# Splitting the first load of an im2col kernel into 2 KB and 6 KB per partition, both ahead of the opening barrier

## The chip, the cores and the metric

The kernel runs on one core of one Trainium2 chip. The metric is device time in microseconds (us), as a median of several executions. The profile's span is shorter than that time by 1.8 us. The rounds ran on different chips; the kernel before had medians of 91.27 to 91.48 us in all of them. "ScalarE" is the engine that the profile calls ACT, "VectorE" is DVE, "SyncE" is SP; SyncE issues every transfer of this kernel. A load or the store of one channel is 128 packets, one for each partition; in the traces sixteen are under way at a time, one on each of sixteen DMA engines, and each engine takes eight.

Times of packets, here, in the prediction and in the expectations, are counted from the trace's last packet of the kind "instruction", which comes 0.07 to 0.09 us ahead of the profile's zero. To compare one of them with a time of the timelines, take off that much.

## The reference

The reference copies every 3 x 3 patch of an input of 16 x 64 x 32 x 32 float32 numbers into columns. Each output row is one shifted 30 x 30 window of one input channel, so the kernel does no arithmetic.

```python
for b in range(batch):
    col_idx = 0
    for i in range(h_out):
        for j in range(w_out):
            patch = x[b, :, i:i + kernel_size, j:j + kernel_size].copy()
            cols[b, :, col_idx] = patch.ravel()
            col_idx += 1
```

It reads 4.19 MB and writes 33.18 MB.

## The kernel before

Each of the 128 partitions holds eight channels of one image, 32 KB. Row r of the flat view below is 32 numbers, or 128 bytes; channel 0 is rows 0 to 31. The first load brings channels 0 and 1 (8 KB a partition), the second the other six (24 KB).

```python
first = load(nc.sync, 0, 2 * H)
load(nc.sync, 2 * H, CPP * H)
...
for c in range(0, CPP, 2):
    out_tile = out_pool.tile([P, 2, KK, HO, WO], x.dtype, name="out_tile")
    for s in range(2):
        for kk in range(KK):
            ki, kj = divmod(kk, K)
            src = in_tile[:, c + s, ki : ki + HO, kj : kj + WO]
            dst = out_tile[:, s, kk]
            if kk % 3 != 1 if c + s == 0 else on_act[n % len(on_act)]:
                nc.scalar.copy(out=dst, in_=src)
            else:
                nc.vector.tensor_copy(out=dst, in_=src)
            n += 1
        if c == 0:
            nc.sync.dma_start(out=out_v[:, s], in_=...)   # one store per channel
    if c > 0:
        nc.sync.dma_start(out=out_v[:, c : c + 2]..., in_=...)
```

So ScalarE copies six of the nine windows of channel 0, and the first store goes out when these and VectorE's three are done. After the program is built, the first load is moved ahead of the barrier that opens the program, at which the engines wait for each other before their own work starts:

```python
at = next(k for k, i in enumerate(head)
          if i.engine == load.engine and type(i).__name__ == "InstDrain")
head.insert(at, load)
```

Nothing in the source mentions ScalarE's table load (the instruction ACT_TABLE_LOAD in the profile). The compiler inserts it in front of ScalarE's first copy.

## Time and profile before

| | before |
|---|---|
| time, median of 6 | 91.30 us (91.22 to 91.51) |
| span of the profiled execution | 89.5 us |
| DMA queue busy | 97.2% of sixteen engines' span |
| VectorE, ScalarE busy | 25%, 31% |
| table load on ScalarE | 0.79 to 2.07 us |
| first copy, first store issued | 4.74 us, 9.92 us |

The lines themselves are in the prediction.

### The profile page before, as it was taken

How to read it: one execution, taken by the hardware profiler on the slowest of the kernel's cores; microseconds unless marked ns; L12 is line 12 of the kernel's file. 1: busy time of each engine (PE TensorE's matmuls, PEld its weight loads, DVE VectorE, ACT ScalarE, POOL GpSimd, SP SyncE). 2: the span in 40 equal slices, each digit the busy share in tenths (PEclk: the TensorE clock that was granted, in tenths of full speed). 3: DMA queues.
4: the chain of work that ended last, by engine and by line, in shares of the span. 5: the costliest groups of instructions: out<-in, count | busy, mean ns of one | idle time of the engine just before them, and what ended most of it. 6: DMA issues, size and time to landing. Idle time of an engine off the chain costs nothing.

```text
span 89.5 us, 136 instructions
## 1 busy us (share of the span) xinstructions
DVE 22.4 (25%) x41; ACT 27.7 (31%) x32; POOL 0.2 (0%) x4
## 2 busy tenths in 40 slices
DVE  0089369900000099400000499200000000000000
ACT  5089999910000099900000499200000000000000
POOL 0000000000000000000000000000000000000000
DMA  5989899999989999996699999999999996779990
GB/s 146 498 373 505 351 463 463 463 463 434 405 376 405 695 463 463 463 405 290 290 405 463 463 463 463 463 463 463 463 463 463 463 463 290 318 318 463 463 463 0
DMA packets 1008, 37.37 MB, mean 417 GB/s; under 512 B 112, under 2 KB 112, under 8 KB 112
## 3 DMA queue, kind: packets, MB, share of 16 engines
q1 hardware_dynamic: 1008, 37.37, 97.2%
HBM read 4.19 MB, written 33.18 MB: 417 GB/s over the span
## 4 chain that ended last, share of the span: by engine, by line
DMA 41%; ACT 15%; DVE 6%; DVEq 1%; issue 0%
DMA out_dram<-out_tile 36%; ACT out_tile L54 15%; DVE out_tile L56 6%; DMA in_tile<-in_x_dram 5%; DVEq L82 1%; DVEq L56 0%
## 5 line engine op out<-in xcount | busy, mean ns | idle before, releaser
L54 ACT COPY out_tile<-in_tile 128x900 f32<-128x900 f32 x31 | 26.5, 938 | 28.0 <-DMA out_dram<-out_tile 25.4
L56 DVE COPY out_tile<-in_tile 128x900 f32<-128x900 f32 x41 | 22.4, 624 | 34.2 <-DMA out_dram<-out_tile 27.1
L54 ACT ACT_TABLE_LOAD x1 | 1.3, 1283 | 0.8 <-PEq L111 0.8
L111 POOL MEMSET const-bfloat16-1.0<- 128x1 bf16 x1 | 0.1, 102 | 0.0
L111 POOL MEMSET const-uint8-127<- 128x1 uint8 x1 | 0.1, 102 | 0.0
L111 POOL MEMSET const-float32-1.0<- 128x1 f32 x1 | 0.1, 99 | 0.0
L111 POOL MEMSET const-float32-0.0<- 128x1 f32 x1 | 0.1, 98 | 0.2 <-issue 0.2
## 6 DMA issues: line engine op xcount, KB each, us to landing
out_dram<-out_tile SPq DMA_DIRECT2D x3, 8100.0 KB, 32.1
out_dram<-out_tile SPq DMA_DIRECT2D x2, 4050.0 KB, 15.3
in_tile<-in_x_dram SPq DMA_DIRECT2D x1, 3072.0 KB, 11.2
in_tile<-in_x_dram SPq DMA_DIRECT2D x1, 1024.0 KB, 4.7
```

Source lines behind the costliest of these rows:

```text
L54: nc.scalar.copy(out=dst, in_=src)
L56: nc.vector.tensor_copy(out=dst, in_=src)
L82: tc.compile()
L111: nc = _bacc.Bacc("TRN2", target_bir_lowering=False, num_devices=1)
```

## The change

The intent is to have a small first piece land sooner, so that work can begin sooner, with both pieces issued ahead of the barrier.

```diff
-    first = load(nc.sync, 0, 2 * H)
-    load(nc.sync, 2 * H, CPP * H)
+    cuts = [0, 16, 2 * H, CPP * H]
+    first = [load(nc.sync, r0, r1) for r0, r1 in zip(cuts[:2], cuts[1:3])]
+    load(nc.sync, cuts[2], cuts[3])
...
-    load = first.ins
...
+    for load in (f.ins for f in first):
...          # each is moved ahead of the barrier, in this order
```

More of the change, by code (lines that the diff above doesn't have):

```diff
@@ L83 @@
     blocks = tc.nc.main_func.blocks
-    load = first.ins
-    home = next(b for b in blocks if any(i.name == load.name for i in b.instructions))
-    home.instructions = [i for i in home.instructions if i.name != load.name]
-    head = list(blocks[0].instructions)
-    at = next(
-        k
-        for k, i in enumerate(head)
-        if i.engine == load.engine and type(i).__name__ == "InstDrain"
-    )
-    head.insert(at, load)
-    blocks[0].instructions = head
+    for load in (f.ins for f in first):
+        home = next(
+            b for b in blocks if any(i.name == load.name for i in b.instructions)
+        )
+        home.instructions = [i for i in home.instructions if i.name != load.name]
+        head = list(blocks[0].instructions)
+        at = next(
+            k
+            for k, i in enumerate(head)
+            if i.engine == load.engine and type(i).__name__ == "InstDrain"
+        )
+        head.insert(at, load)
+        blocks[0].instructions = head
 _INS = ['x', 'kernel_size']
```

## The prediction

> **What bounds the kernel now.** I began with the page, at its rows over time and its DMA queue, because a kernel that moves 4.19 MB in and 33.18 MB out and computes nothing but copies is most likely bound by transfers.
>
> ```profile
> DVE  0089369900000099400000499200000000000000
> ACT  5089999910000099900000499200000000000000
> DMA  5989899999989999996699999999999996779990
> q1 hardware_dynamic: 1008, 37.37, 97.2%
> ```
>
> The reader is to see that VectorE and ScalarE are idle most of the time, that one queue carries everything, and that its packets fill 97.2% of sixteen engines' span. A digit below 9 in the DMA row is not a hole: packets are booked where they end, so slices with few ends look poor. To find real holes I read the timeline of the first 25 us and the DMA issues.
>
> ```profile
> 0.00 1.12 SPq L35 DMA_DIRECT2D in_tile<-in_x_dram  x2
> 0.79 1.28 ACT L54 ACT_TABLE_LOAD   x1 [0.79 <-PEq L111]
> 4.74 13.60 ACT L54 COPY out_tile<-in_tile 128x900 f32<-128x900 f32 x16 [2.67 <-DMA in_tile<-in_x_dram]
> 4.74 4.93 DVE L56 COPY out_tile<-in_tile 128x900 f32<-128x900 f32 x9 [4.74 <-DMA in_tile<-in_x_dram]
> 9.92 2.87 SPq L59 DMA_DIRECT2D out_dram<-out_tile  x2
> 18.36 0.33 SPq L64 DMA_DIRECT2D out_dram<-out_tile  x1
> ...
> in_tile<-in_x_dram SPq DMA_DIRECT2D x1, 3072.0 KB, 11.2
> in_tile<-in_x_dram SPq DMA_DIRECT2D x1, 1024.0 KB, 4.7
> ```
>
> The first load (8 KB a partition, 1024 KB) is issued at 0.00 and has landed at 4.71. The second (24 KB a partition) is issued at about 0.79 and lands 11.2 later, at 12.0. ScalarE loads its table from 0.79 to 2.07 while it would have to wait for the first load anyway, and then copies. The first store is issued at 9.92, when six ScalarE copies and three VectorE copies of channel 0 are done: the issuing queue waited for ScalarE, since VectorE needs only 3 x 0.62 us. The single packet records of the trace complete the picture: the first packet of the first load starts at 1.116 and its last one ends at 4.448; the packets of the second load run out, engine by engine, between 11.285 and 11.717; the first packet of the first store starts at 11.291; the last packet of the last store ends at 88.31. In each DMA engine one packet starts where the one before it ended, across all seven transfers.
>
> So the span is 1.12 (issue to first packet) + 87.19 (engines never empty) + 1.2 (receipt and closing barrier) = 89.5 us. A saving must start the first packet earlier or make packets faster. A loss arises as soon as the queue runs dry, and the place where that is nearest is the seam between the second load and the first store. The store is issued at 9.92. On an empty queue the first load took 1.116 from issue to first packet, so the store could have started at 9.92 + 1.12 = 11.04; the first engine is free at 11.29. The slack is 0.25 us.
>
> **What the Trainium skill says.** "DMA: Bandwidth & Descriptors", section "Issuing engines are not separate DMA queues": all transfers interleave on the same 16 engines. The trace agrees: transfers follow each other without a hole, so cutting one of them adds no bandwidth. The same page, "Latency and other measured facts", gives some 600 ns to the first byte on this path; the trace has 1.116 us for the first load, and I use the trace, with the page's figure as the favourable end. "ScalarE: Activation LUTs", section "What ACT_TABLE_LOAD costs", gives 1283 ns for the table load and a further drain of about 1380 ns for a switch:
>
> ```profile
> L54 ACT ACT_TABLE_LOAD x1 | 1.3, 1283 | 0.8 <-PEq L111 0.8
> ```
>
> The 1283 ns agree. Whether a drain follows the load cannot be seen here, because the engine waits for data after it. "Perfetto Trace Analysis", section "Identifying Dependency Chains", says that an instruction which waits for several engines may get EventSemaphore instructions in front of it with the other conditions. The program before has none ahead of the first ScalarE copy; the changed program has one, and that decides my prediction.
>
> **The change part by part.** (1) It adds one issue on SyncE ahead of the opening barrier: 0.38 us from the two issue durations of the line (0.332 and 0.382). The barrier and the issue of the 24 KB load come some 0.36 us later, at about 1.15 instead of 0.79. The queue still has the first 8 KB to move until 4.45, so this is hidden.
>
> (2) It adds 128 packets and 16 completion packets. A 24 KB packet takes 914 ns, an 8 KB packet 309 ns once running: 3 x 309 - 914 is 13 ns for two more packets, so some 6 ns each. Each engine gets 8 more: 0.05 us, plus 0.01 for its completion packet. I put 0.1 us on the landing of all loads: the 6 KB piece lands at 4.8, the 24 KB load is out of the engines from 11.39.
>
> (3) It does not let a copy start sooner. The first copies read rows 0 to 29 of channel 0; the small piece holds rows 0 to 15. So both engines' first copies wait for both pieces, and the last bytes that they need come no earlier than before.
>
> (4) It moves a wait. In the instruction order of the changed program the first ScalarE copy has two loads to wait for. The wait for the 6 KB piece has become an instruction of its own, and it stands ahead of the table load; the copy itself keeps only the wait for the 2 KB piece. Before, the table load waits for nothing but the barrier, and the copy for the load. So the 1.28 us of table load, which lay inside the wait of 4.74, now come after the landing. ScalarE starts copying at 4.8 + 0.05 + 1.28 = about 6.1, against 4.74.
>
> (5) The first store follows ScalarE. From first copy to issue took 9.92 - 4.74 = 5.18 us; that stays. So it is issued at 6.1 + 5.18 = 11.3, and with 1.12 to the first packet it starts at 12.4, while the first engine is empty at 11.39. The hole is 1.0 us with 1.12 of latency, 0.5 us with the page's 0.6. I take 0.9. The slack of 0.25 is eaten before it: delay 1.36 less 0.25 is 1.1, plus or minus the 0.1 by which the loads themselves end later, which is the same sum.
>
> (6) A restart may ramp. The first load's packets took 369 ns on average against 309 in the steady state, eight to an engine: 0.48 us lost. A store into HBM need not do the same; I put 0.05 to 0.1 on it.
>
> (7) Later stores are not on the path. The second is issued at 12.5 + 1.3 = 13.8 and the engines have the first one until about 22; the third goes from 18.36 to 19.7 with work until about 31. Both later output tiles are released by stores and get the same shift.
>
> Sum: 0.1 for the packets, 0.9 for the hole, 0.1 for the restart: 1.1 us on 91.28, so 92.4.
>
> **The rivals.** Hidden or neutral, 91.3: the table load might be executed ahead of the wait all the same, or the engines' queues might hold enough. For it speaks that a 97% busy queue hides most things; against it that the wait is an instruction in ScalarE's own order and that the seam has only 0.25 us of slack. A small gain, 91.0: smaller first packets could get through the slow ramp at the start (500 to 900 ns for many of the first 8 KB packets) faster. For it speaks that this ramp costs 0.48 us; against it that the bytes are the same and that the first packet cannot start before 1.12. A long table switch, 93.7: if the drain of 1.38 us follows the table load before the first copy, the hole grows to 2.3 us. Against it speaks that no drain stands in the program between the two. A double loss at the start: if the second piece's descriptors come too late, the small piece (256 KB, 0.6 us at the steady rate) is through before them. The second issue lies 0.38 us behind the first, so its first packet can start at 1.5, and the small piece lasts till 1.7 at the earliest: no hole, 0.1 at worst.
>
> **Range and chances.** The sum is 1.1 with about 0.5 us of uncertainty from the latency and 0.3 from the restart; the neutral rival has perhaps one chance in ten and sets the lower end, the drain rival also one in ten and sets the upper. Two per cent is 1.83 us, so slower needs 93.1. A gain of 2% would need 1.8 us out of a start that has 1.1 before the first packet: almost excluded. I give 92.4, 91.6 to 93.1.
>
> **What would show it right or wrong.** In the profile after, the table load should start at about 4.8, released by a load, and the first ScalarE copy at about 6.1; VectorE's first copy should stay at 4.7 to 4.9. The first store should be issued at about 11.3, and the fine windows from 11.4 to 12.4 should show engines with nothing to do. All later landings should be shifted by the same 1 us. If the table load still starts near 1 us, step 4 is wrong; if it is late and no hole appears, steps 5 and 6 are; if ScalarE starts a microsecond or more after the table load's end, the drain is real.

## The result, and the profile after

| | before | after |
|---|---|---|
| time, median of 6 | 91.30 us (91.22 to 91.51) | 92.65 us (92.21 to 93.01) |
| span of the profiled execution | 89.5 us | 90.4 us |

The ratio is 1.0146, with a 95% interval of 1.0114 to 1.0177. Ratios here are worked out from the fast runs of the same rounds, so they are not quite the ratios of the medians quoted. The changed kernel is 1.35 us slower by the medians. It also scatters more: 0.8 us from its fastest to its slowest execution, against 0.3 us. The profiled execution was the fastest one.

These are the rows over time and the queue of the page after; each digit is the busy share of a fortieth of the span, in tenths.

```profile
DVE  0089329930000079700000299400000000000000
ACT  0089999970000079930000299400000000000000
DMA  5989897999999939999999999999999639999990
q1 hardware_dynamic: 1152, 37.37, 96.6%
```

ScalarE's row begins with 00, where it began with 50: the work that it used to do at the very start has gone from there. The queue has 144 packets more (1008 before). The timeline of the first 25 us, with the landing times from the DMA issues, shows where the work went (columns: start, duration, engine, line, operation, and in brackets how long the engine idled and what ended that).

```profile
0.00 1.59 SPq L35 DMA_DIRECT2D in_tile<-in_x_dram  x3
...
4.93 1.28 ACT L55 ACT_TABLE_LOAD   x1 [4.93 <-DMA in_tile<-in_x_dram]
4.96 4.93 DVE L57 COPY out_tile<-in_tile 128x900 f32<-128x900 f32 x9 [4.96 <-DMA in_tile<-in_x_dram]
6.23 13.61 ACT L55 COPY out_tile<-in_tile 128x900 f32<-128x900 f32 x16
11.42 2.87 SPq L60 DMA_DIRECT2D out_dram<-out_tile  x2
12.93 6.01 DVE L57 COPY out_tile<-in_tile 128x900 f32<-128x900 f32 x11 [3.04 <-DMA in_tile<-in_x_dram]
...
in_tile<-in_x_dram SPq DMA_DIRECT2D x1, 3072.0 KB, 11.6
in_tile<-in_x_dram SPq DMA_DIRECT2D x1, 768.0 KB, 4.4
in_tile<-in_x_dram SPq DMA_DIRECT2D x1, 256.0 KB, 2.6
```

The table load now starts at 4.93, when a load has landed; it waited 0.79 for the barrier before. The 2 KB piece has landed by 2.6, but nothing could use it. ScalarE's copies start at 6.23 instead of 4.74 and the first store is issued at 11.42 instead of 9.92. VectorE's second stretch starts when the 24 KB load has landed: that is 12.93 here and was 12.02.

The chain of waits (start, duration, what) names the same piece:

```profile
4.88 0.02 ACTq L55
4.90 0.03 issue
4.93 1.28 ACT L55
6.22 0.01 issue
6.23 13.62 ACT out_tile L55 x16
```

ACTq at 4.88 is the separate wait for the 6 KB piece; behind it stands the table load, and behind that the copies. The chain is not to be read as a sum of the loss. It goes on through ten more ScalarE copies that the first store does not need, and it does not show that the DMA engines were still busy with loads for a good part of that time.

For that I used the trace's single packet records. The first row below is before, the second after; the columns are explained under the table.

| kernel | mean, longest 24 KB packet (ns) | engines out of the loads | first packet of the first store | last engine starts the first store | time of that execution |
|---|---|---|---|---|---|
| before | 915, 1094 | 11.29 to 11.73 | 11.29 | 11.72 | 91.32 |
| after | 925, 1212 | 11.55 to 12.65 | 12.34 | 12.65 | 92.21 |

"Engines out of the loads" gives the first and the last of the sixteen engines to finish its 24 KB packets. Before, each engine's first store packet follows its last load packet at once. After, fourteen of the sixteen are out between 11.55 and 11.95 and wait until 12.34 to 12.49 for the store: that is the hole of the prediction. The other two come out at 12.58 and 12.65 and do not wait at all. These two had stood without a packet between the 6 KB and the 24 KB piece: they began their 24 KB packets at 5.31 and 5.32, the other fourteen by 4.63. Once an engine has started its first store, it works without a pause to the end, and each has the same bytes to move. From the last engine's start of its first store to the end of the execution's time it is 79.6 us in both (91.32 - 11.72 and 92.21 - 12.65). In all fourteen traces this difference lies between 79.5 and 79.7 us. So one number explains the time: when the last of sixteen engines starts its first store. An engine does so at the later of two moments, when its loads are done or when the store's packets reach it.

Two causes can therefore be at work, and the fastest execution alone cannot tell which makes the median of 92.65, where by this rule the last engine starts near 92.65 - 79.6 = 13.05.

### The profile page after: what moved, and what is told of

Its sections match the earlier page's. It is cut to its first block, busy times and chain, and to the rows that moved or that the text cites. A ratio compares the mean times of both kernels' runs of the same rounds, so it can differ in the third digit from the quotient of the medians.

```text
span 90.4 us, 140 instructions
## 1 busy us (share of the span) xinstructions
DVE 22.4 (25%) x41; ACT 27.8 (31%) x32; POOL 0.2 (0%) x4
## 4 chain that ended last, share of the span: by engine, by line
DMA 40%; ACT 16%; DVE 6%; DVEq 1%; SPq 0%; issue 0%; ACTq 0%
DMA out_dram<-out_tile 35%; ACT out_tile L55 15%; DVE out_tile L57 6%; DMA in_tile<-in_x_dram 5%; ACT L55 1%; DVEq L83 1%; SPq L35 0%; DVEq L57 0%; ACTq L55 0%
## 5 line engine op out<-in xcount | busy, mean ns | idle before, releaser
L55 ACT ACT_TABLE_LOAD x1 | 1.3, 1283 | 4.9 <-DMA in_tile<-in_x_dram 4.9
```

## The experiments

My theory was the one of the prediction: the separate wait holds the table load back, and the first store comes too late. The rival that I took up first was that the split itself costs.

**e1_table_first** places the table load by hand, ahead of every wait.

```diff
+    nc.scalar.preload_act_table(mybir.ActivationFunctionType.Copy)
```

> The split stays; the table load is placed by hand ahead of the wait, as one instruction at the start of ScalarE's program. Theory (the late table load delays the first store until the DMA engines have run dry): the table load runs from about 1.1 to 2.4 us, the first ScalarE copy starts at 4.9, the first store is issued at 10.1 and its first packet follows the loads without a hole; 91.3 to 91.5 us. Rival (the split itself costs: 128 more packets, one more issue, slower loads): still 92.4 to 92.8 us. Mixed: whatever is left over 91.3 is the split's own part.

It took 92.05 us (91.75 to 93.00), ratio 1.0093. The timeline of the first 25 us:

```profile
1.26 1.28 ACT L45 ACT_TABLE_LOAD   x1 [1.26 <-PEq L116]
5.27 13.61 ACT L57 COPY out_tile<-in_tile 128x900 f32<-128x900 f32 x16 [2.72 <-DMA in_tile<-in_x_dram]
...
10.46 2.87 SPq L62 DMA_DIRECT2D out_dram<-out_tile  x2
12.51 6.01 DVE L59 COPY out_tile<-in_tile 128x900 f32<-128x900 f32 x11 [2.30 <-DMA in_tile<-in_x_dram]
```

The table load is hidden again and no engine waits more than 0.1 us for the store, but over half of the loss is still there. The 24 KB load lands at 12.5 instead of 12.0.

**e2_six_then_two** swaps the sizes, so that channel 0 lies in the first piece and each copy waits for one load.

```diff
-    cuts = [0, 16, 2 * H, CPP * H]
+    cuts = [0, 48, 2 * H, CPP * H]
```

> The same two pieces in the other order, 6 KB and then 2 KB, so that all rows of the first copies lie in the first piece and each copy waits for one load. Same number of issues and packets as the changed kernel. Theory: no wait ahead of the table load, first ScalarE copy a little before 4.7 (the 6 KB land earlier than 8 KB), first store issued at 9.3 to 9.9, 91.3 to 91.5 us; the earlier store buys nothing, since the queue is still full of loads then. Rival (the split itself costs): 92.4 to 92.8 us.

It took 93.32 us (92.85 to 93.44), ratio 1.0209: both sides of my expectation missed it, and the theory alone is refuted.

```profile
1.25 1.28 ACT L55 ACT_TABLE_LOAD   x1 [1.25 <-PEq L114]
4.25 7.69 ACT L55 COPY out_tile<-in_tile 128x900 f32<-128x900 f32 x9 [1.72 <-DMA in_tile<-in_x_dram]
...
9.44 2.87 SPq L60 DMA_DIRECT2D out_dram<-out_tile  x2
14.16 6.01 ACT L55 COPY out_tile<-in_tile 128x900 f32<-128x900 f32 x7 [2.21 <-DMA in_tile<-in_x_dram]
```

Everything on the copying side is earlier than in the kernel before: the copies start at 4.25 and the store is issued at 9.44. Yet the 24 KB load lands at 14.1. Thirteen engines are out of the loads by 12.11, the other three at 13.68 to 13.90, and the time follows those three.

**e3_unsplit_table_late** is the kernel before, with the table load made to wait for the one first load.

```diff
+    table = nc.scalar.preload_act_table(mybir.ActivationFunctionType.Copy)
+    tc.add_manual_dep(table.ins, first.ins.name, ...)   # a wait for the first load
```

> The kernel before, not split, but its table load is made to wait for the first load. Theory: table load from 4.75 to 6.03, first store issued at 11.2, its first packet at 12.1 to 12.3 while the engines are free from 11.29 to 11.72; a hole of 0.5 to 0.8 us and 91.9 to 92.2 us, that is most of the loss without any split. Rival (the split itself costs): 91.3 us.

It took 91.89 us (91.84 to 92.07), ratio 1.0065, a hit. The profile:

```profile
4.82 1.28 ACT L44 ACT_TABLE_LOAD   x1 [4.82 <-DMA in_tile<-in_x_dram]
...
6.11 13.60 ACT L61 COPY out_tile<-in_tile 128x900 f32<-128x900 f32 x16
11.30 2.87 SPq L66 DMA_DIRECT2D out_dram<-out_tile  x2
12.10 6.00 DVE L63 COPY out_tile<-in_tile 128x900 f32<-128x900 f32 x11 [2.33 <-DMA in_tile<-in_x_dram]
```

The loads are as quick as before (landing at 12.1) and all sixteen engines wait for the store, whose packets start at 12.24 to 12.39. So the late table alone costs 0.57 us (91.89 - 91.32, the median of the kernel before in these rounds), with little scatter.

**e4_waits_swapped** keeps the split and the order on the queue, but names the 6 KB load first in the program, so that the separate wait in front of the table load is the one for the 2 KB piece.

```diff
-    first = [load(nc.sync, r0, r1) for r0, r1 in zip(cuts[:2], cuts[1:3])]
+    second = load(nc.sync, cuts[1], cuts[2])
+    first = [load(nc.sync, cuts[0], cuts[1]), second]
```

> The split and the order of the transfers stay; the two loads stand in the other order in the program, so that the wait ahead of the table load is the one for the 2 KB piece and the copy keeps the one for the 6 KB piece. Theory: the table load starts at about 2.6 us when the small piece has landed, ends at 3.9 and is hidden; first copy at 4.9, 91.3 to 91.5 us. Rival 1 (the split itself costs): 92.4 to 92.8 us. Rival 2 (it is the extra wait instruction as such, or a drain after a table load, that costs): over 92 us.

It took 91.86 us (91.50 to 92.96), ratio 1.0054 without the slow 92.96. The table load ran from 2.68 to 3.96 and was hidden, the store was issued at 10.19. The extra wait as such, then, makes no hole; which piece it waits for decides. As in e1 (0.73 us), part of the loss stays (0.54 us), with the last engine out of the loads at 12.31.

These four show two causes: the hole (e3), and engines that come late out of the loads when the first load is cut (e1, e2, e4). Most of the next ones ask about the second.

**e5_four_four** cuts in the middle.

```diff
-    cuts = [0, 16, 2 * H, CPP * H]
+    cuts = [0, 32, 2 * H, CPP * H]
```

> After the first four runs the loss has two parts: the hole at the first store (unsplit with a late table 0.57 us) and engines that end their loads late when the first load is cut (table early, still 0.5 to 0.7 us; 6 and then 2 KB even 2.0 us). Here the cut is at 4 KB, so channel 0 is whole in the first piece and no wait stands ahead of the table load. If any cut in the first load spreads the engines: last engine free of loads later than 12.1 us, 91.8 to 93.3 us. If it is the small 2 KB piece: engines free between 11.3 and 11.8 as before and 91.3 to 91.5 us.

It took 93.54 us (93.48 to 93.89), ratio 1.0245, above even the higher expectation and the worst of the useful kernels. The copies start at 3.57, the store is issued at 8.76, and the 24 KB load lands only at 14.2:

```profile
3.57 7.70 ACT L55 COPY out_tile<-in_tile 128x900 f32<-128x900 f32 x9 [1.04 <-DMA in_tile<-in_x_dram]
...
14.21 6.01 ACT L55 COPY out_tile<-in_tile 128x900 f32<-128x900 f32 x7 [2.94 <-DMA in_tile<-in_x_dram]
```

So the 2 KB size is not needed for it. A 24 KB packet takes 912 ns when undisturbed; here 54 of 128 take over 1000 ns and the longest 2052.

**e6_scalar_four** is the changed kernel with its late table, but ScalarE copies four windows of channel 0 instead of six, which lets the store go out early.

```diff
-                if kk % 3 != 1 if c + s == 0 else ...
+                if kk in (0, 2, 4, 6) if c + s == 0 else ...
```

> The changed kernel with its late table load, but ScalarE copies four of the nine patches of channel 0 instead of six, so the first store can be issued although the table is late. If the late table costs only through the hole: store issued at 6.2 + 4 x 0.85 = about 9.7 us, no hole, and the time falls to that of the kernel with the table loaded first, 91.8 to 92.1 us. If a late table costs in another way too: 92.4 us or more.

It took 92.63 us (91.83 to 93.13), ratio 1.0133. The store was issued at 9.82, as meant, and the traced execution had no hole and took 91.83. The median missed my expectation: it is that of the changed kernel. Closing the hole lowered the fastest execution (92.21 to 91.83), not the median.

**e7_second_load_split** leaves the first load whole and cuts 2 KB from the second.

```diff
-    load(nc.sync, 2 * H, CPP * H)
+    load(nc.sync, 2 * H, 2 * H + 16)
+    load(nc.sync, 2 * H + 16, CPP * H)
```

> The first load stays whole; a 2 KB piece is cut from the second load instead (8, 2 and 22 KB). As many issues, packets and completions as the changed kernel, the table load early. If it is the number of packets, of loads or the small packets that makes engines end late: 91.8 us or more. If it is the cut in the first load, where the engines are still starting up: 91.3 to 91.5 us.

It took 91.79 us (91.69 to 92.56), ratio 1.0058, at the border of the two expectations. Engines were out of the loads at 11.67 to 12.21, against 11.29 to 11.73. A cut elsewhere costs as well, about as much as the 2 and 6 KB cut does with a hidden table. So the extra load may cost something wherever it stands, but the counts of packets and loads, the same in e2 and e7, do not explain the 2 us of e2.

**e8_one_ahead** has the table first and only the 2 KB piece ahead of the barrier.

```diff
-    first = load(nc.sync, 0, 2 * H)
+    first = load(nc.sync, 0, 16)
+    load(nc.sync, 16, 2 * H)
+    nc.scalar.preload_act_table(mybir.ActivationFunctionType.Copy)
```

> The split of the change with the table loaded first, but only the 2 KB piece ahead of the opening barrier; the 6 KB piece is issued after it. If two issues ahead of the barrier (a later barrier and a later 24 KB load) made the engines end late: 91.3 to 91.5 us. If it is the split: 91.8 to 92.5 us like the kernel with the table loaded first, perhaps a little more from a gap between the two pieces near 1.8 us.

It took 91.73 us (91.64 to 92.04), ratio 1.0050. That is a little less than e1 (92.05) and e4 (91.86), whose ranges overlap it, and still above the kernel before. The place of the second issue is at most a small part. The 24 KB load was still issued at 1.18 us (1.27 in the changed kernel, 0.79 before), so its later issue is not tested. No 24 KB packet was long here (940 ns at most): the delay arose before them.

**e9_copies_after_loads** asks whether the copies slow the loads. It is e5 with the table first and every copy held until the 24 KB load has landed. Its time is bad on purpose.

```diff
+                if n in (0, 1):      # the first copy of each engine
+                    tc.add_manual_dep(copy.ins, last.ins.name, held)
```

> 4 and 4 KB as in the worst kernel so far, but no copy begins before the 24 KB load has landed. The time is bad on purpose (first store issued 5.2 us after that landing, about 98 us); what is asked is how the 24 KB packets fare with no copy beside them. If copies running while the loads start are what slows the packets: all but the first few 24 KB packets take 912 ns and the engines end within 0.6 us of each other, near 11.3 to 11.9. If the cut by itself slows them (how sixteen engines read the input together): many packets of 1.0 to 2.0 us and the last engine near 14, as with the copies.

It took 99.62 us (99.46 and 99.78).

```profile
13.52 11.91 ACT L58 COPY out_tile<-in_tile 128x900 f32<-128x900 f32 x14 [10.98 <-DMA in_tile<-in_x_dram]
```

No copy ran before 13.5, and still 24 of the 128 packets of 24 KB took over 1000 ns, the longest 2159, and the engines came out at 12.10 to 13.20. The kernel before has two such packets. So the cut by itself slows the loads, without copies beside them, though in e5, with copies, there were more of them (54) and the last engine came later (13.97).

**e10_four_four_wait_both** is e5 with the table first and the first copies waiting for both pieces; the edit is that of e9 with `first[1]` in place of `last`.

> 4 and 4 KB, table loaded first, but the first copies wait for both pieces, so they begin at about 4.8 as in the kernel before and not at 3.6. If it is copies that begin before the 24 KB load does: engines end near 11.3 to 12.0, 91.4 to 91.9 us. If it is the cut by itself: last engine near 14, 93.5 us.

It took 92.73 us (92.33 to 92.81), ratio 1.0143. The last engine came out at 13.26, much as in e9 (13.20). The time lies between my two expectations: most of the loss is the cut, and e5, whose copies and first store both come 1.3 us earlier, loses another 0.8 us. Which of the two does that is not told apart.

**e11_unsplit_late_four** tests the hole where no slow loads disturb it: e3 with four windows on ScalarE.

```diff
-            if kk % 3 != 1 if c + s == 0 else ...     # e3
+            if kk in (0, 2, 4, 6) if c + s == 0 else ...
```

> The unsplit kernel with the table made late (91.89 us), and ScalarE copying four patches of channel 0 instead of six. There are no slow loads in this one, so it tests the hole alone. If the late table costs only through the first store: store issued at 6.1 + 4 x 0.85 = 9.6, no hole, 91.3 to 91.5 us. If a late table costs otherwise: 91.8 us or more.

It took 91.31 us (91.17 to 91.45), ratio 0.9998, a hit. The profile:

```profile
4.66 1.28 ACT L44 ACT_TABLE_LOAD   x1 [4.66 <-DMA in_tile<-in_x_dram]
...
9.45 2.87 SPq L66 DMA_DIRECT2D out_dram<-out_tile  x2
11.98 6.00 DVE L63 COPY out_tile<-in_tile 128x900 f32<-128x900 f32 x11 [1.31 <-DMA in_tile<-in_x_dram]
```

The table load is as late as in e3, but the store is issued at 9.45 and each engine goes from its loads to the store without a pause. A late table costs only through the first store.

**e12_changed_again** is the changed kernel itself, for a second trace.

> The changed kernel once more, for a second trace: its first trace was of its fastest execution (92.21 us), in which fourteen engines waited for the first store until about 12.4 us and the slowest two came out of the loads at 12.6. In all traces so far the time is the moment at which the last engine starts its first store plus 79.6 us. If the median of 92.65 us is set by engines that come late out of the loads and not by the hole: in a trace of about 92.6 us most engines start the first store near 12.4, and one or a few near 13.0, straight after their loads. If the hole itself varies: the store is issued late and all engines start near 13.0.

It took 92.89 us (92.82 to 93.06), ratio 1.0158; the traced execution took 92.99.

```profile
4.96 1.28 ACT L55 ACT_TABLE_LOAD   x1 [4.96 <-DMA in_tile<-in_x_dram]
...
11.45 2.87 SPq L60 DMA_DIRECT2D out_dram<-out_tile  x2
13.67 6.00 DVE L57 COPY out_tile<-in_tile 128x900 f32<-128x900 f32 x11 [3.75 <-DMA in_tile<-in_x_dram]
```

Table and store are where they were in the first trace (4.93, 11.42), so the hole does not vary. What varies is the landing of the 24 KB load, 13.67 against 12.93. Fifteen engines start their first store at 12.37 to 12.52. One comes out of its loads at 13.45 and starts straight away; 13.45 + 79.54 is 92.99. In this execution that one engine sets the time. It began its 24 KB packets at 5.94, when the other fifteen had begun by 4.65, and then took 0.91 to 0.92 us for seven of the eight and 1.14 for one: it is late because it stood still between the pieces, and hardly because its packets were slow.

The packet records of the traced executions together:

| kernel | mean, longest 24 KB packet (ns) | engines out of the loads | last engine starts the first store | time of that execution |
|---|---|---|---|---|
| e12, the changed kernel | 941, 1418 | 11.60 to 13.45 | 13.45 | 92.99 |
| e3, unsplit, table late | 914, 1068 | 11.31 to 11.84 | 12.39 | 92.07 |
| e11, the same, no hole | 914, 1052 | 11.24 to 11.70 | 11.70 | 91.27 |
| e1, 2 and 6 KB, table first | 923, 1711 | 11.41 to 12.24 | 12.30 | 91.92 |
| e4, 2 and 6 KB, waits swapped | 917, 1156 | 11.36 to 12.31 | 12.30 | 91.86 |
| e8, 2 KB ahead, table first | 912, 940 | 11.54 to 12.00 | 12.01 | 91.64 |
| e6, 2 and 6 KB, late, no hole | 921, 1172 | 11.41 to 12.25 | 12.24 | 91.83 |
| e7, second load cut (22 KB packets) | 868, 1265 | 11.67 to 12.21 | 12.21 | 91.76 |
| e2, 6 and 2 KB | 990, 2087 | 11.83 to 13.90 | 13.90 | 93.44 |
| e5, 4 and 4 KB | 1092, 2052 | 12.33 to 13.97 | 13.97 | 93.53 |
| e10, the same, wait for both | 989, 1888 | 11.88 to 13.26 | 13.26 | 92.81 |
| e9, the same, no copies | 996, 2159 | 12.10 to 13.20 | 19.78 | 99.46 |

None of these beats the kernel before. e11 equals it.

The packet records also show where engines stand still. Between 1.7 and 6.0 us of the profile, before, e3 and e11 have sixteen packets under way all the time: the gaps of all engines together are 0.01 us at most. In every kernel with a cut there are gaps, 0.3 us (e2) to 3.4 us (e10) in sum over the engines, 2.2 us in the trace after and 2.3 us in e12. In these two, most of it falls on the engines that then come last. In e2, e5 and e9 the engines that come last have long packets instead, of up to 2.1, 2.1 and 2.2 us.

## Why the prediction was right or wrong

The outcome held most likely (slower, but within 2%) came about, and 92.65 lies in 91.6 to 93.1, and the loss is 1.35 us where 1.1 was forecast. Its reason holds only in part, and that the sum came so near is partly luck: the hole was put too high, and engines that come late out of the loads, which the prediction does not have, made up for it.

- Step 1 (one more issue) was a little low: the 24 KB load was issued at 1.27, not 1.15. Whether that is quite hidden is not tested.
- Step 2 failed: "I put 0.1 us on the landing of all loads". The 24 KB load landed 0.9 us later in the fastest execution and 1.65 us later in the second trace. The step counted a fixed cost per packet, the same for every engine. That part is of the right size: the packets of the first 8 KB took 3.07 us of an engine on average after, 2.95 before. What it lacks is single engines that stand still between the 6 KB and the 24 KB piece: two of them begin the latter some 0.7 us after the rest in the trace after, one 1.3 us after the rest in e12. Longer 24 KB packets (up to 1.4 us instead of 0.91) add only 0.1 and 0.2 us to the mean engine there.
- Step 3 (no copy starts sooner) is right: the 2 KB piece landed at 2.6 and the first copy, VectorE's, started at 4.96, against 4.74.
- Step 4 (the moved wait holds the table load back) is right, and shown: the table load went from 0.79 to 4.93, 4.8 being forecast. So the rival that it is hidden all the same falls; and as ScalarE's copies started 0.02 us after the table load's end, the drain rival falls too.
- Step 5 (the hole) is right in kind; e3 makes it without any split and e11 takes it away again with the table still late. It was mis-sized. Forecast at 0.9 us, it costs 0.57 us alone. The step counted from the first free engine; the last engine sets the end, and it had 12.39 - 11.72 = 0.67 us to lose. And from the store's issue to its first packet it was 0.84 to 0.85 us (after, e12, e3, e9, with both times on the profile's clock), not 1.12.
- Step 6 (a restart ramp of up to 0.1 us) is right in size: in the trace after, the first store's packets took 1213 ns on average against 1200, eight to an engine, which is 0.1 us. In e3 and e9, where all engines restart, the time is the last start plus 79.68 us, about 0.1 more than elsewhere (79.54 to 79.63). The two engines that set the end in the trace after did not restart, so there it is not in the time.
- Step 7 is right: the second and third store were issued at 13.95 and 19.86 (13.8 and 19.7 forecast), and no engine was without a packet after its first store began.
- The final sum failed too: it adds the terms. An engine starts its store at the later of "loads done" and "store there", so the late loads and the hole hide each other. The hole sets a floor for the changed kernel of about 12.5 + 79.6 = 92.1 us, near its fastest execution. In the second trace a late engine set the time above that floor, and the medians of 92.65 and 92.89 point the same way. In e6 the floor was gone and the median was not clearly better.
- The gain rival (small packets pass the ramp faster) falls: both pieces had landed at about 4.86, the single load at 4.71. The rival of a hole between the two pieces falls as well: from 1.7 to 2.6 us of the profile, where the 2 KB packets run out, the gaps in the trace after are 0.05 us in sum over sixteen engines.

Three slips of its working change little. It adds packet times, which are counted from 0.09 us ahead of the profile's zero, to times of the timeline: the first packet started 1.03 us after the issue and not 1.12, but as both sides of the seam carry the same 0.09, the slack of 0.25 us stays. Packets are booked where they start and not where they end: the last store's packets, which end at 88.2 us of the profile, stand in the window from 85 to 86 us (busy share 2.40, 0.00 from 86 to 88). And the upper end of the range is the 2% line of 93.1, not the drain rival's 93.7.

What stays open is why, after a cut, engines stand still between loads and some later packets take long. The runs show that it needs neither copies beside it (e9) nor a late table (e1, e4, e7). They make the counts of packets and loads (e7) and the place of the second issue (e8) at most a part. The later issue of the last load (1.17 to 1.27 us in every kernel with a cut, 0.79 before) is untested. In every trace with a 24 KB packet over 1000 ns, the longest is among the first sixteen of its load, before as well, so the way in which sixteen engines fall into step while they read the input may be the cause; that is argued, not shown. Also open is why e6, with a late table, has a worse median (92.63) than e1 and e4 (92.05 and 91.86), whose tables are early: their traces look alike, and no trace of a slow execution of e6 exists. They ran on another chip. On e6's own chip, the changed kernel (e12) has a ratio of 1.0158 (1.0143 to 1.0172) and e6 one of 1.0133 (1.0098 to 1.0168), so a small gain is not excluded.

## What to carry to other kernels

When a copy gets a second load to wait for, look in the instruction order for what the extra wait now stands in front of; a table load that was hidden may end up behind the data, and loading the table by hand at the start, or changing which of the two waits comes first, undoes that. In a kernel whose DMA engines are always busy, ask for the last engine and not for the mean: a piece that lands early buys nothing, and the later of "loads done" and "store's packets there" on the slowest engine sets the time. The split load was not free here even where its landing was hidden, so measure such a change with several executions, look at their scatter, and look in the packet records for engines that stand still.

## What the Trainium skill lacked or had wrong

- "Perfetto Trace Analysis", section "Identifying Dependency Chains", tells of waits put in front as instructions of their own. It lacks that ScalarE's table load can stand behind such a wait: here it moved from 0.79 to 4.93 us.
- "ScalarE: Activation LUTs", section "What ACT_TABLE_LOAD costs", adds a drain of some 1380 ns to every switch to a different set. Here, at the first table load of the program, the copies follow 0.02 us after its end (6.21 and 6.23); the 1283 ns agree.
- "DMA: Bandwidth & Descriptors", section "Latency and other measured facts", gives about 600 ns to the first byte. From the start of the issuing instruction to the first packet the runs show 1.00 to 1.03 us for the first load, and 0.84 to 0.85 us for a store that found waiting engines; from its end, 0.62 to 0.65 and 0.50 us. The page lacks from where it counts.
- "Perfetto Trace Analysis", section "DMA Optimizations", says that splitting may help if the engines are generally idle. No page has what a split costs where they are busy: here engines stand still between the pieces (0.3 to 3.4 us in sum over sixteen, 0.01 at most without a cut), they leave the loads 0.46 to 2.07 us apart (0.44 before), and the time follows the last, by 0.4 to 2.2 us with no hole.
